# Reordering a two-layer streaming encoder into one-sequence blocks, with 64-row score pairs and denominators from ones columns beside V

## The chip, the cores and the metric

The kernel runs on one Trainium2 chip, on all 8 cores. Each core computes 2 of the 16 sequences and no core talks to another. The metric is device time in microseconds (us) of the slowest core. TensorE (PE in the profile) does the matmuls, VectorE is DVE, ScalarE is ACT, GpSimd is POOL and SyncE is SP.

Executions fall into two states. In the fast state the eight cores agree within about 0.5%. In the slow one, the cores of one or both dies show a lower granted TensorE clock and the run takes some per cent longer. Everything below compares fast runs, or the cores of an undisturbed die, unless it says otherwise.

## The reference

The model dimension is 1,024 and a sequence has 2,048 positions. In order: FFN, mixer A, FFN, FFN, mixer B, FFN. Cut and simplified to what matters:

```python
def rms_norm(x, g):
    y = x * lax.rsqrt(jnp.mean(x * x, axis=-1, keepdims=True) + EPS)
    return y * g
...
for layer in range(DEPTH):                       # DEPTH = 2
    h = h + 0.5 * swiglu(rms_norm(h, ffn1_norm[layer]), ...)      # hidden 2816
    hn = rms_norm(h, mix_norm[layer])
    if layer < N_A_LAYERS:                       # layer 0
        # 16 heads of 64; chunks of 64 see themselves and 8 chunks back,
        # with a bias by clipped relative distance
        h = h + chunked_relpos_attention(hn, ...)
    else:                                        # layer 1
        # 8 heads; scores = 128-row part + 64-row rotary part, block-causal
        h = h + mla_attention(hn, ..., k_nope, k_rope, v_shared, cos, sin)
    h = h + 0.5 * swiglu(rms_norm(h, ffn2_norm[layer]), ...)
    if layer == N_A_LAYERS - 1:
        # latent (256) and rotary key (64) from one norm of h, up-projected per head
        k_nope, k_rope, v_shared = mla_shared_kv(rms_norm(h, kv_norm), ...)
return rms_norm(h, final_norm)
```

## The kernel before

Activations lie transposed, model dimension on the partitions, in tiles of 512 positions; four tiles are a sequence. A stage runs over both sequences before the next stage starts. A small scheduler keeps one instruction list per engine, in program order, and puts a semaphore wait wherever data demands it. Program order on TensorE therefore decides what can hide what.

A norm is a load of 2 MB, one square of 4,096 columns on ScalarE, eight matmuls against a matrix of ones (which sum over partitions and spread the sum over all of them), two ScalarE steps, and eight VectorE products:

```python
def norm_core(x3, xR, C, gcol, out3, outR, n, sq, defer=None):
    ...
    sch.add('act', lambda e: e.activation(sq3[:, 0:C, :], x3, AF.Square), [xR], [sqR])
    ps, psR = P[7]
    for c in range(C):
        MM(ps[:], ones[:], sq3[:, c, :], c == 0, c == C - 1, [sqR, onesR], [psR])
    ...   # rs = exp(-0.5 * ln(ps / n + eps)), then out = x * gain * rs
```

Inside an FFN stage the norms of the second sequence hide in the first one's down projection. At the start of a stage, and of each mixer, they hide in nothing:

```python
# in a_stage (mixer A), setup
for sbl in range(4):
    load_norm(src, srcR, t0 + sbl, G_MIX[0], st['hn'][:, :, sbl * 512:(sbl + 1) * 512],
              st['hnR'][sbl], st['sq'])
```

Both mixers multiply the exponentials by V and then, in a second matmul of the same width, by ones, for the softmax denominators. This is mixer A; one projection bank (`P[1]`; a bank is one of the eight accumulators of 128 x 512 that the kernel allots to TensorE's results) serves all query, key and value groups, and each group is copied out before the next may start:

```python
def pv_(u):
    ...
    MM(po[:, c0:c1], v3[:, kt, :], pT[:, c0:c1], first, last, [vR, pTR], [poR])
    MM(pd[:, c0:c1], ones[:], pT[:, c0:c1], first, last, [onesR, pTR], [pdR])
    if last:
        RCP(rd_[pl, :], pd[pl, :], [pdR], [rdR], 'dve' if hh == 0 else 'act')
        ...   # ao = po * rd_
```

A head of mixer A has 64 rows. Its scores are computed with 128 rows by filling the other head's half of the query tile with zeros; B's rotary part does the same. Per head, B projects keys, values and queries with nothing else on TensorE, then runs its attention. The output projection follows as a separate step with a residual load and store of 1 MB per group of four.

The softmax here doesn't subtract the row's maximum and nothing guards it: scores larger than these inputs give would overflow.

## Time and profile before

| | before |
|---|---|
| first six runs | 7126.6 to 7717.8 us, median 7267.9 |
| profiled run | 7131.0 us, cores 7081 to 7130 us |
| matmuls per core | 29,858, streaming 13.41 M columns |
| start-to-start spacing, 512 / 128 columns | 216 / 55.6 ns |

The spacing comes from the order of time of the trace. It agrees with the Trainium skill, "TensorE: Matmul & The Clock Gate", Part 1 ("Wait — 56ns, not 53.3ns?"): columns divided by 2.4 GHz plus about 2.5 ns. That formula is used below to say how much time a list of matmuls *must* take; I call this work. Before: 13.41 M / 2,400 per us + 29,858 × 2.5 ns = about 5,660 us. The remaining 1,470 us of 7,131 are waits, and time lost to half clock after waits.

First the page of the profile before. The second line is busy time per engine, the third the granted clock in 40 slices in tenths, the last the chain that ended last.

```profile
span 7129.5 us, 85828 instructions; the slowest of 8 cores (7081.2 to 7129.5 us)
PE 5934.0 (83%) x29282; PEld 2774.7 (39%) x29856; DVE 1893.9 (27%) x2488; ACT 1819.8 (26%) x2947; POOL 364.6 (5%) x1502
...
PEclk9999998997999899998999998799979997999897
...
PE 59%; DMA 21%; DVE 8%; ACT 6%; issue 4%; SPq 1%; POOL 0%; DVEq 0%; ACTq 0%; POOLq 0%; another core or an unknown queue 0%
```

PE reads 83% busy, but it counts the tail of each matmul's pipeline, so it is more than the work. The chain is the better warning: TensorE explains only 59% of the way to the end, DMA 21%. The clock dips in the slices where mixers start, and in some others. Next, what TensorE waited for (name of what it waited for, microseconds in total, number of waits, longest):

```profile
PE ps L383 <- ACT arena L431: 621.1, 64, 32.7
PE ps L383 <- DVE rr L469: 111.1, 62, 7.7
PE ps L383 <- DVE xn L650: 96.1, 15, 10.1
```

L431 is the square of a norm, L469 the residual add of the FFN, L650 that of a mixer. The squares in turn wait for loads:

```profile
L431 ACT ACTIVATE arena<-xn 128x4096 bf16<-128x4096 f32 (+2 forms) x80 | 261.6, 3270 | 1642.8 <-DMA xn<-xs 1433.8
L390 DVE RECIPROCAL rstd<-ps 64x512 f32<-64x512 f32 x64 | 214.4, 3350 | 106.1 <-PE ps L383 105.7
```

That is 1,434 us of ScalarE idleness ended by a load from DRAM, and a 3.35 us reciprocal, 64 times. Last, four stretches of the trace (span of the window, its length, busy time of PE, PEld, DVE, ACT, POOL, granted clock, DMA share, GB/s):

```profile
71.00:433.00 362.00, 360.21 (x1640) 163.87 (x1672) 73.26 (x106) 58.65 (x92) 12.67 (x24) 1.00 0.31 65
1043.00:1147.00 104.00, 42.20 (x221) 19.65 (x225) 34.63 (x48) 20.80 (x13) 0.53 (x1) 0.69 0.28 90
1147.00:1596.00 449.00, 382.39 (x2946) 228.74 (x3000) 232.08 (x225) 255.03 (x512) 73.08 (x463) 1.00 0.10 22
4386.00:4637.00 251.00, 122.38 (x435) 47.99 (x444) 100.83 (x140) 67.69 (x52) 2.64 (x5) 0.74 0.29 85
```

An FFN up projection keeps TensorE full (360 of 362 us at clock 1.00). The start of a mixer A sequence has it 42 of 104 us at clock 0.69, that of B's 122 of 251 at 0.74. This is where the time lies.

### The profile page before, as it was taken

What the parts mean: (1) busy time and instruction counts of PE and PEld (TensorE: products, weight loads), DVE (VectorE), ACT (ScalarE), POOL (GpSimd) and SP (SyncE); (2) the same over time, 40 slices, a digit from 0 to 9 for tenths busy, and PEclk for the clock granted to TensorE, in tenths of its full rate; (3) what the DMA queues carried; (4) which work ended last, traced back from release to release, by engine and by line L of the source; (5) the groups of instructions that cost most, each with busy time, mean ns of one, the idle gap of its engine ahead of it and who ended that gap; (6) DMA issues with size and microseconds to landing.
All of it is one profiled execution on the core that took longest, in us unless ns stands there. A gap on an engine that the chain in (4) does not pass through costs nothing.

```text
span 7129.5 us, 85828 instructions; the slowest of 8 cores (7081.2 to 7129.5 us)
## 1 busy us (share of the span) xinstructions
PE 5934.0 (83%) x29282; PEld 2774.7 (39%) x29856; DVE 1893.9 (27%) x2488; ACT 1819.8 (26%) x2947; POOL 364.6 (5%) x1502
## 2 busy tenths in 40 slices
PE   6999977885887799997998996588847886998795
PEld 2444433542553344443443442244313442443342
DVE  2222114552553212111212112322242112112212
ACT  2111103551553211110211111255324551111201
POOL 0000000110111000000000000000000000000000
PEclk9999998997999899998999998799979997999897
DMA  4242251014013425225325234211331116244335
GB/s 105 41 130 55 52 131 39 19 25 148 19 34 87 113 40 134 51 56 140 70 56 131 39 74 125 68 28 27 101 128 24 28 32 180 39 84 124 99 76 156
DMA packets 220021, 553.57 MB, mean 78 GB/s; under 512 B 18640, under 2 KB 18640, under 8 KB 211408
## 3 DMA queue, kind: packets, MB, share of 16 engines
q1 hardware_dynamic: 171936, 375.49, 16.4%
q0 software_dynamic: 47664, 172.54, 14.8%
q8 instruction: 254, 4.16, 0.2%
q14 instruction: 167, 1.37, 0.1%
HBM read 603.05 MB, written 117.44 MB: 101 GB/s over the span
## 4 chain that ended last, share of the span: by engine, by line
PE 59%; DMA 21%; DVE 8%; ACT 6%; issue 4%; SPq 1%; POOL 0%; DVEq 0%; ACTq 0%; POOLq 0%; another core or an unknown queue 0%
PE ps L383 59%; DMA rr<-xs 10%; DMA xn<-xs 4%; DMA rr<-xT 4%; ACT arena L431 2%; DVE rr L469 2%; DVE arena L449 2%; DMA xs<-xn 2%; ACT arena L777 1%; SPq L393 1%; DVE rstd L390 1%; ACT arena L992 1%; ACT arena L955 1%; DMA xn<-xT 1%; ACT rstd L440 0%
## 5 line engine op out<-in xcount | busy, mean ns | idle before, releaser
L383 PE MATMUL ps<-arena,wbf 128*128 128x512 bf16 (+1 forms) x20430 | 4629.1, 384 | 370.3 <-DVE rr L469 111.1
L383 PEld LDWEIGHTS ps<-arena,wbf 128*128 128x128 bf16 (+1 forms) x20864 | 2047.6, 99 | 2893.5 <-issue 587.1
L383 PE MATMUL ps<-arena,ones_sb 128*128 128x512 bf16 (+3 forms) x2100 | 711.2, 383 | 636.9 <-ACT arena L431 621.1
L383 PE MATMUL ps<-arena 128*128 128x512 bf16 (+3 forms) x3584 | 882.2, 325 | 129.0 <-POOL arena L782 32.9
L512 DVE TENSOR_TENSOR arena<-sg,ps 128x512 bf16<-128x512 f32 x704 | 483.1, 687 | 1896.4 <-PE ps L383 1837.7
L510 ACT ACTIVATE sg<-ps 128x512 f32<-128x512 f32 x704 | 420.4, 597 | 2009.0 <-PE ps L383 1906.0
L431 ACT ACTIVATE arena<-xn 128x4096 bf16<-128x4096 f32 (+2 forms) x80 | 261.6, 3270 | 1642.8 <-DMA xn<-xs 1433.8
L383 PEld LDWEIGHTS ps<-arena 128*128 128x128 bf16 x3712 | 358.2, 98 | 529.7 <-issue 278.7
L777 ACT ACTIVATE arena<-ps,cvec_sb 128x512 bf16<-128x512 f32 (+3 forms) x896 | 432.0, 525 | 458.7 <-PE ps L383 429.9
L383 PEld LDWEIGHTS ps<-arena,ones_sb 128*128 128x128 bf16 x2112 | 217.5, 105 | 816.1 <-issue 745.2
L449 DVE SCALAR_TENSOR_TENSOR arena<-xn,gains_sb,rstd 128x512 bf16<-128x512 f32 x512 | 384.2, 750 | 493.1 <-ACT rstd L442 450.8
L469 DVE SCALAR_TENSOR_TENSOR rr<-ps,rr 128x512 f32<-128x512 f32 x256 | 177.1, 692 | 1204.6 <-DMA rr<-xs 824.9
L409 POOL DMA_DIRECT2D wbf<-wblob x330 | 174.3, 528 | 5005.7 <-PE ps L383 4828.1
L992 ACT ACTIVATE arena<-ps 128x512 bf16<-128x512 f32 (+3 forms) x640 | 326.0, 531 | 189.1 <-PE ps L383 183.7
L390 DVE RECIPROCAL rstd<-ps 64x512 f32<-64x512 f32 x64 | 214.4, 3350 | 106.1 <-PE ps L383 105.7
L383 PE MATMUL ps<-arena,ident_sb 128*128 128x256 bf16 (+1 forms) x608 | 153.4, 254 | 34.0 <-DVE arena L736 31.5
L1012 DVE TENSOR_TENSOR arena<-ps,rstd 128x512 bf16<-128x512 f32 x64 | 44.3, 692 | 515.2 <-ACT rstd L388 509.3
L383 PE MATMUL ps<-wbf,arena 128*128 128x128 bf16 x2560 | 167.8, 222 | 9.3 <-DVE arena L708 7.7
L383 PEld LDWEIGHTS ps<-wbf,arena 128*128 128x128 bf16 x2560 | 154.9, 99 | 40.3 <-issue 19.5
L650 DVE TENSOR_TENSOR xn<-ps,xn 128x512 f32<-128x512 f32 x128 | 88.5, 691 | 255.1 <-PE ps L383 130.2
L440 ACT ACTIVATE rstd<-ps,eps_sb 128x512 f32<-128x512 f32 x80 | 55.0, 687 | 300.0 <-PE ps L383 289.1
L801 DVE TENSOR_TENSOR arena<-ps,rstd 64x512 bf16<-64x512 f32 x128 | 88.2, 689 | 137.2 <-ACT rstd L388 130.5
(38 smaller groups left out, 1022.2 us busy)
## 6 DMA issues: line engine op xcount, KB each, us to landing
xn<-xs SPq DMA_DIRECT2D x56, 2048.0 KB, 9.5
wbf<-wblob POOLq DMA_DIRECT2D x216, 512.0 KB, 5.2
xs<-rr SPq DMA_DIRECT2D x256, 256.0 KB, 2.5
rr<-xs SPq DMA_DIRECT2D x192, 256.0 KB, 4.0
wbf<-wblob POOLq DMA_DIRECT2D x64, 704.0 KB, 7.1
xn<-xs SPq DMA_DIRECT2D x32, 1024.0 KB, 6.9
xs<-xn SPq DMA_DIRECT2D x32, 1024.0 KB, 9.1
xn<-xT SPq DMA_DIRECT2D x8, 2048.0 KB, 10.1
```

The source lines that it names most:

```text
L383: sch.add('pe', lambda e: e.matmul(out, lhsT, rhs, start=start, stop=stop), rd, wr)
L390: sch.add('dve', lambda e: e.reciprocal(out, in_), rd, wr)
L409: sch.add('pool', lambda e: e.dma_start(out=wb[:, 0:w], in_=src), [], [wbR], 'wq%d' % bi)
L431: sch.add('act', lambda e: e.activation(sq3[:, 0:C, :], x3, AF.Square), [xR], [sqR])
L449: sch.add('dve', lambda e: e.scalar_tensor_tensor(out3[:, c, :], x3[:, c, :], gains[:, gcol + c:gcol + c + 1], rs[:], ALU.mult, ALU.mult), ...
L469: sch.add('dve', lambda e: e.scalar_tensor_tensor(r[:], po, scale, r[:], ALU.mult, ALU.add), [poR, rR], [rR])
L510: sch.add('act', lambda e, sgt=sgt, pg=pg: e.activation(sgt[:], pg[:], AF.Silu), [pgR], [sgR])
L512: sch.add('dve', lambda e, av=av, sgt=sgt, pu=pu: e.tensor_tensor(av, sgt[:], pu[:], ALU.mult), [sgR, puR], [st['actR'][s]])
L650: sch.add('dve', lambda e, r=r, po=po: e.tensor_tensor(r, po[:], r, ALU.add), [poR, xR], [xR])
L777: sch.add('act', lambda e: e.activation(pT[:, c0:c1], sp_[:, c0:c1], AF.Exp, bias=cvec[:, h:h + 1]), [spR, cvR], [pTR])
L801: sch.add('dve', lambda e: e.tensor_tensor(ao[pl, a, QB * 512:(QB + 1) * 512], po[pl, :], rd_[pl, :], ALU.mult), [poR, rdR], [st['aoR'][QB]])
L992: sch.add('act', lambda e: e.activation(pT[:, c0:512], sp_[:, c0:512], AF.Exp, scale=scale), [spR], [pTR])
```

## The change

The intent has four parts:

1. **One-sequence blocks.** The order becomes F0 F0 A A F1 F1 F2 F2 B B F3 F3, each block one sequence (FFN of sequence 0, FFN of sequence 1, and so on), written F00, F01, A0, A1, F10, … below. The norm of block n+1 runs as background steps in the tail of block n: beside the down projection of an FFN, beside the last head and output projection of a mixer. B's shared latent and rotary key are made in the tails of F11 and F20 ("KV blocks").
2. **Row-tiled scores.** A's two heads of 64 rows go to the two halves of the array as a pair, and so do B's rotary parts of two key tiles. No zero padding.
3. **Denominators for free.** A's V tile for one head is 64 columns of V and 64 of ones, so one matmul gives both. B turns its product over: the exponentials are the stationary operand, V with a ones column (129 columns) streams past, and the result, query-major, is transposed back.
4. **Projection of the next head inside the current one**, in small groups between attention units; output projections by tile, with 256 KB residual loads and stores through a ring of four buffers.

The core of the diff (2,086 lines in all):

```diff
@@ the norm of the next block as a list of steps @@
+        def norm_steps(jobs, overlap=True):
+            ...
+            for n, j in enumerate(jobs):
+                ...
+                if n < 2:
+                    out.append(j.load)
...
@@ ffn_block, down projection @@
+            kv = blk in KV_IN
+            if next_jobs:
+                bg.q = norm_steps(next_jobs)
...
+                        rs.add(i, t0 + s, po, poR, 0.5)
+                        bg.step(4 if kv else 2)
...
@@ the KV steps of a norm job @@
+                if kv:
+                    tail += [knrm(0), knrm(1), knrm(2), knrm(3), nop, kmm(0), kmm(1), krope, ksq, nop, kst, kfin]
...
@@ mixer A, scores @@
-                        MM(sp_[:, c0:c1], kT[:, kt * 128:(kt + 1) * 128], qT[:, hh, QB * 512 + c0:QB * 512 + c1],
-                           True, not has_g, [kR, qR], [spR])
...
+                for hh in range(2):
+                    sp_, spR = P[b0_ + hh]
+                    pl = slice(hh * 64, hh * 64 + 64)
+                    MM(sp_[:, c0:c1], k_[ks][0][pl, kc:kc + 128], q_[QB][0][pl, c0:c1], not has, True,
+                       [k_[ks][1], q_[QB][1]], [spR], skip=True)
...
@@ mixer A, product with V @@
-                        MM(po[:, c0:c1], v3[:, kt, :], pT[:, c0:c1], first, last, [vR, pTR], [poR])
-                        MM(pd[:, c0:c1], ones[:], pT[:, c0:c1], first, last, [onesR, pTR], [pdR])
...
+                for hh in range(2):
+                    po, poR = P[4 + hh]
+                    MM(po[:, c0:c1], va[:, kt % 4, hh, :], pt[:, hh, c0:c1], first, last, [vr, ptR], [poR])
+                if last:
+                    rd_, rdR = rstd[nxt('rstd', 2)]
+                    ACT(rd_[0:64, :], P[4][0][64:128, :], AF.Ln, [P[4][1]], [rdR])
+                    ACT(rd_[64:128, :], P[5][0][0:64, :], AF.Ln, [P[5][1]], [rdR])
+                    ACT(rd_[:], rd_[:], AF.Exp, [rdR], [rdR], scale=-1.0)
...
@@ mixer B, product with V, query-major @@
+                    for qt in range(max(k - 4 * Q, 0), 4):
+                        po, poR = P[4 + qt // 2]
+                        cc = (qt % 2) * 256
+                        MM(po[:, cc:cc + 129], pt[:, i, qt * 128:(qt + 1) * 128], vh[k // 4][0][:, k % 4, 0:129],
+                           k == 0 and qt % 2 == 0, k == 4 * Q + qt, [vh[k // 4][1], ptR], [poR], skip=True)
...
@@ residual ring @@
+                dma(xview(dst, i, sb), r[:], [rR], [dstR[sb][i]], 'rs%d' % k)
+                self.ahead(self.order.index((i, sb)) + 4)
```

## The prediction

> **What bounds it now.** TensorE is busy 5934 of 7130 us (first part of the page), which counts pipeline tails. The order of time shows a 512-column matmul starting every 216 ns, a 128-column one every 55.6 ns. The 29,858 matmuls stream 13.41 M columns, so TensorE needs about 5,660 us. The other 1,470 us are waits, plus half clock after them (948 us at 0.5 in the clock record). The waits view: TensorE waits 621 us for squares of norms (which wait for loads), 111 us for FFN residual adds, 96 us for mixer residual adds. The stage windows: FFN runs at pace (first one 972 us against 925 of work); mixer A takes about 1,275 us against 865 of work, mixer B 1,580 against some 1,000. Norms and projections around the head loops run TensorE 40 to 55% busy at clock 0.7 to 0.78.
>
> **What changes, counted from both instruction lists.**
> 1. Columns fall to 12.61 M: the ones matmuls for denominators go (A 287 k, B 279 k; B's query-major product adds 2 k and 33 k of transposes); the rotary query's two 64-column passes become one. Same spacings: 5,330 us, 330 less.
> 2. A's scores and B's rotary scores become 64-row pairs. If pairs run side by side (the Trainium skill, "TensorE: Matmul & The Clock Gate", Part 3, says row tiles do; no run here shows it), 282 k columns vanish: -118 us. But "TensorEngine Tiling (Array Packing)", Key Properties, says that changing tiling mode drains TensorE. This trace agrees: switching between 128*128 and 128*64 matmuls spaces 310 ns, not 216: 94 ns more. 768 units x 2 switches x 94 ns = +144 us. Net about zero.
> 3. Norms, KV projection and output projections move into tails or beside the last head. Their sources are already stored, blocks being ordered by sequence. Most of the 621, 111 and 96 us and the half clock goes.
> 4. Exponentials cover two heads or key tiles (from 594 ns per 512 columns to an estimated 1.02 us per 1,024); 3.35 us reciprocals go.
>
> **New costs.** A has one output bank pair, freed after Ln, Ln, Exp and two multiplies, about 3.9 us; two projection groups (3.5 us) cover it. Output projection loads follow their stores on one queue with four buffers, so back-to-back groups take about 2.7 us instead of 1.73: 10 to 15 us per mixer block. The KV chain has five dependent hops per tile: 5 to 8 us x 8.
>
> **Sum (estimate).** Start 55; FFN 3,700 with norms; KV 14 + 50; A 2 x 440; B 2 x 450; final tail 12; about 5,620 us undisturbed. The before median is 2% above its fastest runs; I allow a little for that.
>
> Predicted: 5650 us, range 5450 to 5900. Faster by over 2%: 0.97; within 2%: 0.02; slower: 0.01.
>
> **What shows it right.** Waits for norm squares under 60 us; half clock under 150 us; FFN blocks of 455 to 480 us; A near 440 and B near 450 us per sequence; row pairs starting within 10 ns of each other, 94 ns lost per mode switch; the chain of waits almost all TensorE.
>
> **What would make it wrong.** Row pairs that do not overlap (+118 us); dearer switches (each 100 ns more is +154 us); weight loads of the query-major product not hidden[...]; background DVE or ACT work holding up exponentials; denser TensorE work that lowers the granted clock (at 0.94 throughout, +350 us).

## The result, and the profile after

The changed kernel takes 5920.6 us (median of ten runs; the eight fast ones are 5911.8 to 5926.6 us). Beside it the kernel before took 7170.9 us (median of 20 runs). The ratio is 0.8294, with a 95% interval of 0.8273 to 0.8315. Ratios here are the mean time of one kernel's fast runs over that of the other's in the same rounds, so not quite the ratio of the medians.

So it is 17% faster, and still 270 us slower than predicted, 21 us above the range.

The same four parts of the page, after:

```profile
span 5916.7 us, 83304 instructions; the slowest of 8 cores (5889.9 to 5916.7 us)
PE 5500.0 (93%) x29784; PEld 2580.6 (44%) x29784; DVE 1785.1 (30%) x2784; ACT 1571.7 (27%) x2313; POOL 293.4 (5%) x1053
...
PEclk9999999999999999999999899999998999999999
...
PE 83%; DMA 5%; DVE 5%; ACT 3%; issue 2%; SPq 0%; DVEq 0%; ACTq 0%; POOL 0%; POOLq 0%
```

The chain is now TensorE for 83%, and the clock is full nearly everywhere. What TensorE still waits for:

```profile
PE ps L381 <- ACT sq L384: 147.3, 28, 35.5
PE ps L381 <- DVE arena L396: 47.5, 25, 7.2
PE ps L381 <- DVE rr L387: 45.5, 13, 13.3
PE ps L381 <- DVE arena L387: 43.6, 76, 3.0
PE ps L381 <- DVE sq L390: 42.2, 8, 6.9
PE ps L381 <- ACT arena L384: 24.0, 41, 2.4
```

In order: squares of norms, copies of a projection out of its bank, residual adds of the mixers, multiplications (in A those that free the output bank), the products of a KV tile, and exponentials. The 621 us of squares became 147, of which 35.5 is the very first load of the program. The residual adds of the FFN are no longer among the larger waits.

### Accounting by block

I split each block's span by the spacing from start to start of the matmul records: *work* (columns/2.4 GHz + 2.5 ns, a row pair counted once), *switch* (what a change of tiling mode adds), *cold* (what half clock adds to a spacing), and *wait* (the rest). This is my own arithmetic on the trace, not a view of the profile. A few waits below are sums by this spacing too, which come out up to 0.2 us per wait longer than the waits view (48 us for the residual adds where the view has 45.5; 116 us for squares inside the blocks where it has 111.8).

| block, after | span us | work | switch | cold | wait |
|---|---|---|---|---|---|
| F01, F10, F21, F30, F31 (each) | 466 to 483 | 463 to 470 | 0 | 0 to 3 | 2 to 8 |
| F00 (its span includes 35.5 before the first matmul) | 541 | 470 | 0 | 4 | 32 |
| A0, A1 (each) | 471 | 349 | 44.5 | 8 | 69 |
| F11, F20 (KV; each) | 535, 538 | 485 | 0 | 11 | 39, 43 |
| B0, B1 | 504, 497 | 375 | 32 | 17, 15 | 79, 75 |
| all twelve and the ends | 5,917 | 5,209 | 153 | 81 | 430 + 44 at the ends |

Before, the same arithmetic gives the two A sequences together 879 of work and 360 of wait in 1,272 us, and the two B sequences 1,066 and 415 in 1,565 us (the shared keys are inside B there). These are from core 1, whose trace holds all matmuls; the records of the slowest core lack 574 of them, and what is missing would count as wait.

The KV block's loss can be read in the order of time of the trace, here in F11 (start, duration, engine, line, what it made from what; in brackets idle time before, and what ended it):

```profile
2767.04 6.73 DVE L390 SCALAR_TENSOR_TENSOR sq<-xn,gains_sb,rstd 128x512 bf16<-128x512 f32 x8
...
2774.03 7.51 PE L381 MATMUL ps<-sq,wbf 128*128 128x512 bf16 x24 [5.47 <-DVE sq L390]
...
2783.60 1.48 DVE L387 TENSOR_TENSOR xn<-ps,xn 64x512 f32<-64x512 f32 x2 [9.23 <-DMA xn<-tabT]
2785.18 1.06 ACT L384 ACTIVATE sq<-xn 128x1024 bf16<-128x1024 f32 x1 [4.61 <-DVE xn L387]
...
2786.38 0.59 PE L381 MATMUL ps<-sq,ones_sb 128*128 128x512 bf16 x2
```

Eight products on VectorE take 6.73 us, more than the FFN group of 22 matmuls (4.75 us) that TensorE has beside them, and TensorE waits 5.47 us. After that its 24 matmuls take 7.51 us where 5.2 would do: for the first 4.5 us or so they run at half clock. Then the rotary products at 2783.60 wait for a load of their table, the square at 2785.18 waits for them because it reads the tile that they write, and the sum at 2786.38 waits for the square. That is one tile of eight. Each such handing over from one engine to the next is called a hop below.

The mixer's tail, here the end of A0:

```profile
1453.99 0.37 SPq L378 DMA_DIRECT2D xn<-xs  x1
...
1458.34 0.53 POOL L426 DMA_DIRECT2D wbf<-wblob  x1 [13.63 <-PE ps L381]
...
1461.80 0.53 POOL L426 DMA_DIRECT2D wbf<-wblob  x1 [2.92 <-PE ps L381]
...
1475.41 0.69 DVE L387 TENSOR_TENSOR rr<-ps,rr 128x512 f32<-128x512 f32 x1 [13.18 <-DMA rr<-xs]
...
1476.25 3.57 PE L381 MATMUL ps<-arena,wbf 128*128 128x512 bf16 x8 [13.33 <-DVE rr L387]
```

At 1453.99 a 2 MB load for the next norm is issued. At 1458 and 1461.8 two weight loads are issued on another queue. The residual tile that the add at 1475.41 needs had its load issued at 1456.08; it landed 19 us later, and TensorE stood 13.3 us. The window around it shows what the 16 DMA engines were doing:

```profile
1456.00:1475.00 19.00, 6.92 (x33) 2.94 (x30) 4.11 (x6) 3.59 (x5) 1.05 (x2) 0.81 0.96 234
```

Their busy share is 0.96, at 234 GB/s, while TensorE worked 6.9 of 19 us.

### The profile page after: what moved, and what is told of

It is laid out like the page before. It is cut to its first block, busy times and chain, and to the rows that moved or that the text cites. A ratio compares the mean times of both kernels' runs of the same rounds, so it can differ in the third digit from the quotient of the medians.

```text
span 5916.7 us, 83304 instructions; the slowest of 8 cores (5889.9 to 5916.7 us)
## 1 busy us (share of the span) xinstructions
PE 5500.0 (93%) x29784; PEld 2580.6 (44%) x29784; DVE 1785.1 (30%) x2784; ACT 1571.7 (27%) x2313; POOL 293.4 (5%) x1053
## 4 chain that ended last, share of the span: by engine, by line
PE 83%; DMA 5%; DVE 5%; ACT 3%; issue 2%; SPq 0%; DVEq 0%; ACTq 0%; POOL 0%; POOLq 0%
PE ps L381 83%; DVE hn L390 2%; DMA xn<-xs 2%; ACT rstd L384 2%; DVE arena L387 1%; DMA xs<-rr 1%; ACT sq L384 1%; DMA rr<-xs 1%; DMA xn<-xT 1%; DVE sq L390 1%; DMA xn<-tabT 0%; ACT arena L384 0%; SPq L378 0%; PE ps L1220 0%; DMA hn<-tabT 0%
## 5 line engine op out<-in xcount | busy, mean ns | idle before, releaser
L381 PE MATMUL ps<-hn,wbf 128*128 128x512 bf16 x13440 | 2951.7, 380 | 36.6 <-DVE xn L396 13.6
L381 PEld LDWEIGHTS ps<-hn,wbf 128*128 128x128 bf16 x13440 | 1310.7, 98 | 1600.1 <-issue 67.2
L381 PE MATMUL ps<-arena,wbf 128*128 128x512 bf16 (+1 forms) x6520 | 1449.8, 381 | 66.5 <-DVE rr L387 40.9
L381 PEld LDWEIGHTS ps<-arena,wbf 128*128 128x128 bf16 x6520 | 639.7, 99 | 821.9 <-issue 110.4
L384 ACT ACTIVATE arena<-ps 128x1024 bf16<-128x1024 f32 (+5 forms) x896 | 607.9, 695 | 849.8 <-PE ps L381 796.2
L381 PE MATMUL ps<-arena 128*128 128x129 bf16 (+8 forms) x5248 | 727.5, 283 | 85.4 <-DVE arena L387 38.6
L381 PEld LDWEIGHTS ps<-arena 128*128 128x128 bf16 (+1 forms) x5248 | 306.2, 96 | 494.8 <-issue 426.9
L384 ACT ACTIVATE sq<-xn 128x1024 bf16<-128x1024 f32 (+2 forms) x296 | 274.8, 929 | 586.7 <-DMA xn<-xs 231.2
L390 DVE SCALAR_TENSOR_TENSOR hn<-xn,gains_sb,rstd 128x512 bf16<-128x512 f32 x432 | 323.4, 749 | 130.9 <-ACT rstd L384 100.2
L396 DVE CAST arena<-ps 128x512 bf16<-128x512 f32 x384 | 259.2, 689 | 310.5 <-PE ps L381 303.8
L381 PE MATMUL ps<-wbf,hn 128*128 128x128 bf16 x2048 | 128.0, 222 | 12.3 <-DVE arena L396 12.3
```

What stands on the lines that cost most here:

```text
L381: sch.add('pe', lambda e: e.matmul(out, lhsT, rhs, start=start, stop=stop, skip_group_check=skip), rd, wr)
L384: sch.add('act', lambda e: e.activation(out, in_, func, **kw), rd, wr)
L390: sch.add('dve', lambda e: e.scalar_tensor_tensor(out, a, sc, b, op0, op1), rd, wr)
L396: sch.add(eng, lambda e: e.tensor_copy(out, in_), rd, wr)
```

## The experiments

My theory, after reading the trace: work and mode switches are about as predicted (5,209 + 153 against 5,212 + 144), and the whole error is waiting. The waits fall into five groups: late norm loads, the KV hops, the output bank in A, residual tiles in the mixer tails, and copies at the start of a mixer. Rivals: a switch costs more than its spacing shows (then undoing the row pairs gains); the waits hide other limits behind them (then removing one only moves it); and the tail of a mixer is slow because of bulk loads beside it, or because of the ring that feeds it. Where the expectations say theory A and B, they define them each time for that run. Diffs are against the changed kernel. All kernels that I call correct agreed with the reference within its tolerance.

### 1. Norm loads issued earlier

```diff
+        def hoist(js):
+            for j in (js or [])[:2]:
+                j.load()
+                j.load = nop
...
+                if j == NJ - 4:          # FFN: three weight tiles before the tail
+                    hoist(next_jobs)
...
+                    if a == 6:           # A, and h == 6 in B: one head earlier
+                        hoist(next_jobs)
```

> The first two 2 MB loads of the next block's norms are issued well before the tail (four weight tiles before the end of the up products, or one head before the last) instead of at its beginning; nothing else changes. Theory A (the loads are issued only 10 to 19 us before the first statistics need the squares, and land after 11.5 us, so the squares come late): TensorE's wait for squares of norms falls from 147 us to about 55 (what remains is the start of the kernel), half clock falls by some 30 to 50 us, and the time from 5918 to between 5815 and 5850. Rival B (the squares are late because ScalarE is busy or behind in its order): less than 15 us gained, the waits stay.

Measured: correct. Five of six runs fell in the slow state; the one fast run is 5856.8 us, and the undisturbed dies of the slow ones show 5827 to 5855 us per core, against 5890 to 5917 in the profile after. That is about 61 us less. On an undisturbed core plain FFN blocks fall to 462.7 us with no wait at all, the waits for squares inside the blocks from 116 to 31 us, and time at half clock from 290 to 214 us. The A blocks did not gain: they took 477 and 474 us. The waits view of that undisturbed core (core 1):

```profile
PE ps L381 <- ACT sq L384: 65.2, 17, 36.9
```

So late loads were the cause in FFN blocks. In A there was little to gain: squares end only 9.2 us of the waits of its two blocks in the profile after, and in A0 the first two loads of the next norm were already issued at 1237 and 1238 us for a sum at 1390 us.

### 2. The KV chain spread, one hop per FFN group

```diff
-                    tail += [knrm(0), knrm(1), knrm(2), knrm(3), nop, kmm(0), kmm(1), krope, ksq, nop, kst, kfin]
+                    return head[:4], [[st, nrm(0), nrm(1)], [nrm(2), nrm(3), knrm(0)], [knrm(1), knrm(2), knrm(3)],
+                                      [], [kmm(0), kmm(1), krope], [ksq], [kst, kfin]], None
...
-                        bg.step(4 if kv else 2)
+                        bg.step(1 if kv else 2)
```

> In the two FFN blocks that also make the shared keys and values, the background steps are dealt out one set per down group of 22 matmuls, so that each hop that TensorE waits for (scaled rows, squares of the latent) has a group or more between it and its user; the work is the same. Theory A (the 135 us that the two blocks cost over a plain one, where I had estimated 64, are dependent hops issued with no TensorE work between them): the two blocks fall from 535 and 538 to about 490 to 500 us, the time to between 5825 and 5850. Rival B (VectorE or the queue has not the throughput for the extra work in this tail): under 20 us gained, VectorE is still what TensorE waits for.

Measured: correct, fast runs 5848.6 and 5850.9 us, ratio 0.8182 (0.8167 to 0.8198) against 0.8294. The two KV blocks fell from 535 and 538 us to 499 and 498, and the wait for their products (42.2 us in the profile after) is gone. The hops were the main cause, and an FFN group (4.75 us) between two of them covers them. They were not the only one: run 1, which left the hops as they were, took about 16 us off each of these blocks, so late norm loads had a part in them too.

### 3 and 4. Row pairs undone, in A and in B

```diff
 # A: both heads' query tiles padded with zeros again
-                        CP(q_[s][0], pp, [ppR], [q_[s][1]])
+                        for hh in range(2):
+                            pl = slice(hh * 64, hh * 64 + 64)
+                            CP(q_[s][hh][0][pl, :], pp[pl, :], [ppR], [q_[s][hh][1]])
...
-                    MM(sp_[:, c0:c1], k_[ks][0][pl, kc:kc + 128], q_[QB][0][pl, c0:c1], not has, True,
-                       [k_[ks][1], q_[QB][1]], [spR], skip=True)
+                    MM(sp_[:, c0:c1], k_[ks][0][:, kc:kc + 128], q_[QB][hh][0][:, c0:c1], not has, True,
+                       [k_[ks][1], q_[QB][hh][1]], [spR], skip=True)
```

> Mixer A's scores go back to full 128-row products with a zero-padded query (two copies of 64 partitions each), so there is no row tiling and no mode switch in A; all else is as in the kernel after. Theory A (896 switches of about 100 ns cost 89 us, the pairs save only 60): the time falls by 15 to 35 us, to 5885 to 5905; work in A rises from 349 to about 380 us per sequence, switches go to zero. Rival B (switches are hidden in waits that would be there anyway, so that row tiling is a net gain): the time rises by 30 to 60 us.

Measured: correct, fast runs 5914 to 5945 us, ratio 0.8297 (0.8283 to 0.8311). That is no change, where both theories had expected one: a miss. The profiled run, with both dies at a granted clock of 0.82, can't show where the gain went; it shows only that the switches are gone. What ate it stays open. More copies on VectorE is a guess that no fast trace shows.

```diff
 # B: the second half of the rotary key (rows 64 to 127) set to zero, full 128 rows
-            dma(kr[64:128, :], kr_d[:, t0 * 512:(t0 + 4) * 512], [krR_d[t0 + s] for s in range(4)], [krR2], 'kl1')
+            PSET(kr[64:128, :], 0.0, [krR2])
...
-                    MM(sp_[:, c0s[i]:512], kr[pl, k * 128:(k + 1) * 128], qr[Q][0][pl, c0s[i]:512], False, True,
+                    MM(sp_[:, c0s[i]:512], kr[:, k * 128:(k + 1) * 128], qr[Q][0][:, c0s[i]:512], False, True,
```

> Mixer B's rotary scores go back to 128-row products (the second half of the rotary key rows is zeroed instead of a second copy of the key), no row tiling in B; all else as in the kernel after. Theory A (640 switches of about 100 ns cost 64 us, the pairs save 58): the time changes by less than 12 us, rather down. Rival B (switches hidden in waits): it rises by 30 to 58 us.

Measured: correct, 5910.7 to 5911.2 us, ratio 0.8268 (0.8255 to 0.8281): about 7 us less, as expected. In a B block work rises from 375 to 406 us and switches fall from 32 to 0. The pair saves about what the switch costs.

Together the two say that row tiling was worth nothing here, as the prediction had it ("net about zero").

### 5. A's output bank freed in two halves

```diff
                 if last:
-                    rd_, rdR = rstd[nxt('rstd', 2)]
-                    ACT(rd_[0:64, :], P[4][0][64:128, :], AF.Ln, [P[4][1]], [rdR])
-                    ACT(rd_[64:128, :], P[5][0][0:64, :], AF.Ln, [P[5][1]], [rdR])
-                    ACT(rd_[:], rd_[:], AF.Exp, [rdR], [rdR], scale=-1.0)
                     for hh in range(2):
                         pl = slice(hh * 64, hh * 64 + 64)
+                        dl = slice(64 - hh * 64, 128 - hh * 64)
+                        rd_, rdR = rstd[nxt('rstd', 2)]
+                        ACT(rd_[pl, :], P[4 + hh][0][dl, :], AF.Ln, [P[4 + hh][1]], [rdR])
+                        ACT(rd_[pl, :], rd_[pl, :], AF.Exp, [rdR], [rdR], scale=-1.0)
```

> In mixer A the reciprocals of the two heads are taken one after the other (Ln, Exp, multiply for head 0, then the same for head 1) instead of Ln, Ln, one Exp over both, then two multiplies; one more ScalarE instruction per query block, 64 in all. So the first output bank is free about 1.3 us sooner. Theory A (the 27 us per A block that TensorE waits for the output multiply are the single pair of output banks, freed 3.9 us after the last product while the two filler groups cover only 3.5 us): that wait falls from 53 us in both blocks to under 15, the time to about 5875 to 5895. Rival B (VectorE is behind with the fillers' copies, so that the multiply is late whenever the reciprocal comes): under 12 us gained.

Measured: 5902.2 and 5906.9 us, about 14 us less, but a wrong result. That was my slip: with two buffers used per round, the split overwrites a norm's inverse root that a later step still reads. The order of work on each engine is the intended one, so the time still tells something. It tells against the theory: the wait for the output bank did not fall below 15 us, it *rose*, from 43.6 to 64.4 us by the waits view, while the waits for exponentials fell from 24.0 to 7.0:

```profile
PE ps L381 <- DVE arena L387: 64.4, 64, 4.2
...
PE ps L381 <- ACT arena L384: 7.0, 15, 0.8
```

All eight cores agree (61 to 65 us for the bank, 39 to 44 before). The wait moved from one name to another on the same path.

### 6. The starts of the mixers

```diff
-            bias_make(0)
             for g in proj(0):
                 g()
+            bias_make(0)
...
+            MISC_B = [2, 3, 6, 7]
...
-            g0 = proj(0)
+            g0 = proj(0, MISC_B, 'act')
```

B's first projections use four banks instead of two and are copied out by ScalarE.

> Two changes at the starts of mixer blocks. In A the bias rows, whose load lands 9 us into the block, are scaled after the first projections and not before, so that VectorE's copies of queries and keys are not queued behind that load. In B the copies of the first head's projections go to ScalarE, idle there for 30 us, and the down and first projections use four PSUM banks and not two. Theory A (VectorE's order, not its throughput or TensorE, holds up the starts): A's wait of 7 and 5 us for copies goes, B's of about 27 us per block for copies and down projections falls to under 12; the time to about 5870 to 5890. Rival B (the start of B is bound by the table loads and the rotary chain on VectorE): under 15 us gained.

Measured: correct, 5889.1 and 5890.9 us: 29 us less. A0 fell to 465 us and B0 and B1 to 490 and 486. Copies ended 22.3 us of waits instead of 47.5, but the waits for squares rose by 17 us: part of what is freed at the start is spent again later.

```profile
PE ps L381 <- DVE arena L396: 22.3, 21, 1.4
```

### 7. Norm loads in four pieces, and a residual ring of five

```diff
-                dma(self.x3, xfull(src, sb), list(srcR[sb]), [self.xR], 'xn%d' % k)
+                cc = slice(2 * q, 2 * q + 2)
+                dma(self.x3[:, cc, :], xfull(src, sb)[:, cc, :], srcR[sb][cc], [self.xR[q]], 'xn%d_%d' % (self.k, q))
```

> The norm loads of 2 MB are issued as four of 512 KB, and those of the third and fourth tile of a block one by one behind the steps that free their part of the buffer; rows and bytes are the same. Theory A (the residual loads of 256 KB in the output projection tails wait behind a 2 MB load on the same queue: one took 18.6 us to land at 1454 us and TensorE then waited 13.3 us): TensorE's wait for mixer residual adds falls from 48 us to under 20, waits for squares fall too since the first piece lands early, the time to about 5850 to 5885. Rival B (what I wrote in the prediction: stores before loads on one queue with four buffers limit the pace): those waits stay above 35 us.

Measured: correct, 5860.6 and 5865.1 us: 56 us less, a gain of the expected kind for a different reason. The residual waits were to fall and hardly did (48 to 40 us on the profiled core; over all eight cores the view gives 42 to 46 us before and 38 to 47 after). The gain came from the norms themselves: F00 fell from 541 to 520 us, because the first square can start when a quarter of the load is there, and the waits for squares fell from 147.3 to 108.2 us.

```diff
-        rr = [(sb_alloc("rr%d" % i, [128, 512], F32), R()) for i in range(4)]
+        rr = [(sb_alloc("rr%d" % i, [128, 512], F32), R()) for i in range(5)]
...
-                self.ahead(self.order.index((i, sb)) + 4)
+                self.ahead(self.order.index((i, sb)) + 5)
```

> The ring of residual buffers grows from four to five and loads run five ahead (a sixth does not fit). Theory A (2 MB loads ahead in the queue hold up the residual loads): little is gained, waits for mixer residual adds stay above 35 us of 48, the time within 12 us of 5918. Rival B (the store-before-load pace with four buffers): they fall in proportion, to below 25 us, and the time to about 5885 to 5900.

Measured: correct, 5922.5 and 5968.8 us (the second, which is the profiled one, with a slightly low clock on one die): no gain. The waits of TensorE in that kernel:

```profile
PE ps L381 <- ACT sq L384: 186.5, 31, 36.8
...
PE ps L381 <- DVE rr L387: 13.0, 7, 3.6
```

The residual wait fell from 45.5 to 13.0 us, and the wait for squares rose from 147.3 to 186.5. This core is on the disturbed die; the four cores of the other die show the same, with 15 to 28 us for residuals and 152 to 187 for squares, where the eight cores of the changed kernel have 42 to 46 and 131 to 147. A deeper ring does take much of the residual's wait away, but the squares then wait longer by about as much. That both compete for the same DMA engines is my reading of it; the next but one group of experiments looks at that.

### 8. What hiding the norms is worth

```diff
+            if n and blk[:2] != ('F', 2):
+                cur['misc'] = MISC_A
+                for g in norm_steps(jobs):
+                    g()
...
-                a_block(blk, jobs, src, srcR, dst, dstR, nj)
+                a_block(blk, jobs, src, srcR, dst, dstR, None)
```

Everything else stays, but norms run at the start of their own block, as before the change (F2's stay in the tails, with the KV steps).

> The kernel after with the norms of nine of the eleven later blocks taken out of the tail before them and run at the start of their own block, with nothing beside them (the two blocks that make keys and values keep theirs); same instructions, same columns. Theory A (hiding the norms is the largest part of what the change gained: they cost the kernel before about 55 us per block, 621 us of waits for squares in all): the time rises by 380 to 500 us, to 6300 to 6420, with half clock near 600 us. Rival B (the gain came from fewer columns and a denser head loop, the norms' waits being replaced by waits in the tails): under 200 us lost.

Measured: correct, 6320 to 6326 us: 402 us more, within what was expected.

```profile
PE ps L381 <- ACT sq L384: 506.2, 54, 36.3
```

The waits for squares are back at 506 us, and time at half clock is 669 us. So about 400 of the roughly 1,210 us gained come from moving norms into tails. By the accounting, 451 us come from fewer columns (118 of them the row pairs). The rest, after 150 us are lost to switches, comes from projections, residuals and KV no longer running alone; I did not take these apart one by one.

### 9. The mixer's tail: whose loads are in the way?

First the 2 MB norm loads of the last two tiles are left out in mixer tails. The result is wrong (relative error 0.275).

```diff
-                dma(self.x3, xfull(src, sb), list(srcR[sb]), [self.xR], 'xn%d' % k)
+                if not (sch.tag[:1] in ('A', 'B') and sb % 4 >= 2):
+                    dma(self.x3, xfull(src, sb), list(srcR[sb]), [self.xR], 'xn%d' % k)
```

> Wrong results on purpose: in the tails of the four mixer blocks the third and fourth 2 MB norm load of the next block are left out, so those two norms read what the buffer holds; all else is issued as before. Neither smaller pieces nor a fifth buffer moved the mixer tails: with five buffers the residual waits fell from 48 to 24 us but waits for squares rose by as much. Theory A (in these tails the 16 DMA engines are full: 84% busy at 210 GB/s over the last 46 us of the first A block, 96% at the worst, so the bytes themselves are what TensorE waits for): TensorE's wait for mixer residual adds falls from 48 to under 15 us, the time to 5850 to 5885. Rival B (the residual's own chain of store, load and add sets the pace): the waits stay above 35 us, and under 15 us are gained.

Measured: 5896 to 5904 us, 20 us less; the residual waits fall only from 48 to 39 us. In the trace, residual transfers still take 9 to 18 us to land after three 768 KB weight loads issued within 7 us. So the weight loads matter at least as much as the norm loads. Two more kernels were to hold the weight loads back to the end of the block, one of them with the norm loads left out too:

```diff
-        def w_done(name):
+        def w_done(name, fill=True):
             wstate['free'].append(wstate['at'][name].pop(0))
-            w_fill()
+            if fill:
+                w_fill()
...
             bg.flush()
+            w_fill()
```

> In the tails of the mixer blocks the next block's weight tiles are fetched one (two before the second B block) as the output projection frees its buffers, the others only at the block's end. In the run without tail norm loads the stores and loads of residuals, 2.4 to 5 us to landing until then, took 9 to 18 us from the moment three weight tiles of 768 KB were issued (1457 to 1464 us). Theory A (any bulk load in these tails holds up the residuals; taking one kind away leaves the other): alone it gains little, waits for mixer residual adds 30 to 48 us, time within 20 us of 5918. Rival B (the weight tiles alone are the cause): these waits fall below 15 us, the time to about 5870 to 5885.

> Wrong results on purpose: both at once, no third and fourth norm load in the mixer tails and the weight tiles late. Theory A (bulk loads of either kind hold up the residuals): TensorE's wait for mixer residual adds falls from 48 to under 15 us, more than the two runs give separately, and the time to 5850 to 5880. Rival B (the residual's own chain of store, load and add on one queue, as in my prediction): it stays above 30 us.

Measured: the first 5923.7 us and correct (ratio 0.8283, 0.8252 to 0.8314), the second 5890 and 5901 us (wrong, ratio 0.8244), the same as without the norm loads alone. These are null experiments. The first one's trace shows weight loads issued at 1456, 1459 and 1478 us, where the changed kernel has 1458, 1462 and 1480; the second one's at 1460, 1463 and 1467 us, where the run without norm loads has 1457, 1461 and 1464. They are nearly where they were: the load was moved to the end of POOL's *program order*, but POOL does nothing else then, and the load waited only for its buffer. Order in a list holds nothing back; only a dependency does. So again, with a dependency on the block's last VectorE instruction:

```diff
+            endR = R()
+            endR.lw = sch.ops['dve'][-1]
+            w_fill([endR])
```

> The run with late weights did not do what it said: the fetches stood at the block's end in program order but waited for nothing there, and the trace shows them issued at 1460, 1463 and 1467 us as before. Now they wait for the last VectorE instruction of the block. Theory A (any bulk load in the tails holds up the residuals; the norm loads remain): waits for mixer residual adds 25 to 48 us, the time within 20 us of 5918. Rival B (the weight tiles alone are the cause): waits below 15 us, time 5870 to 5885.

> Wrong results on purpose: no third and fourth norm load in the mixer tails, and the weight tiles really held to the block's end. Theory A (bulk loads of either kind hold up the residuals): no residual transfer in the last 40 us of a mixer block takes over 8 us, TensorE's wait for mixer residual adds falls from 48 to under 15 us, the time to 5850 to 5880. Rival B (the residual's own chain of store, load and add with four buffers): the wait stays above 25 us though the transfers are quick.

Measured: weights held, correct, one fast run of 5909.7 us, 9 us under the profiled run and just under the lowest of the changed kernel's other fast runs (5911.8), so the time alone shows little. Held and without norm loads (wrong), 5878.6 and 5885.3 us (and 5896.0 with a low clock on one die), ratio 0.8242 (0.8212 to 0.8272): 35 us less. The residual line of the waits view, weights held:

```profile
PE ps L381 <- DVE rr L387: 30.3, 15, 7.4
```

and with neither (profiled in the run with the low clock):

```profile
PE ps L381 <- DVE rr L387: 22.5, 13, 3.3
```

From 45.5 us (longest 13.3) to 30.3 and 22.5 (longest 3.3). Over all eight cores of each run it is 42 to 46, 26 to 31 and 19 to 22 us, so the steps are clear of the spread, and of the low clock. The last is neither under 15 us, as theory A had it, nor above 25, as its rival had it. In the last 40 us of the four mixer blocks, 12 of 73 residual transfers took over 8 us to land in the changed kernel, 1 of 95 with neither. So bulk loads on the same DMA engines cause the long gaps and about half of the wait. The other half remains with nothing beside it; it comes in many gaps of up to 3 us, which fits the ring's own pace (a store, then a load, per group), but no run shows that alone. It stays open.

### 10. What worked, together

The version combines 1 (in FFN and B only), 2, 4, 5 (with separate buffers, so correct), 6, 7's pieces, and in its last form weights held in mixer tails.

> All that helped, together: early norm loads before FFN and B tails, the key and value steps spaced, loads in four pieces, both mixer starts, reciprocals head by head (in other tiles than before, which mends the wrong result of that run: a norm's scale factors had been overwritten), B's rotary scores without row tiling. If the gains are separate (61, 69, 55, 29, 14 and 7 us, less some 50 that two of them claim twice, and 15 because A's early loads are left out): about 5735 to 5785 us. If they only pass one wait on to the next: above 5815.

> The best version so far (5715 us) with the weight tiles of the mixer tails late. Theory A: with the norm loads in pieces, the residuals' waits fall from 45 to about 25 us, the time to 5690 to 5710. Rival B: no change within 8 us, or slower, because the next block then waits for its weights.

> The best version so far (5715 us) with the weight tiles held to the end of the mixer blocks. Theory A: the residuals' waits fall from about 50 to about 30 us, the time to 5690 to 5710. Rival B: no change within 8 us, or slower, because the next block then waits for its weights.

Measured: the first form 5715.0 and 5715.1 us and correct (5752 with one die slightly disturbed), 20 us better than the expected 5735 to 5785. The second added the weight edit that holds nothing back, and gave 5711.1 and 5711.6: the same. The last form gave 5696.6 us undisturbed (5730 and 5757 with slightly lower clocks), correct, ratio 0.8041 (0.7987 to 0.8096). The step from 5711 rests on this one undisturbed run. Its 5696.6 us are 3.7% below the changed kernel's profiled run of 5918.3 us; by the ratios, whose fast runs include the two slightly disturbed ones, it is 3.1%.

```profile
span 5695.0 us, 84197 instructions; the slowest of 8 cores (5673.9 to 5695.0 us)
PE 5441.9 (96%) x29784; PEld 2625.3 (46%) x29784; DVE 1765.7 (31%) x2760; ACT 1626.4 (29%) x2401; POOL 296.7 (5%) x1055
...
PEclk9999999999999999999999999999999999999999
```

```profile
PE ps L381 <- ACT sq L384: 61.1, 21, 32.1
PE ps L381 <- DVE arena L387: 59.7, 61, 4.1
PE ps L381 <- DVE rr L387: 31.6, 15, 6.7
PE ps L381 <- DVE arena L396: 29.1, 24, 2.0
```

By the block accounting, waits are 253 us (from 430) and cold is 42 (from 81). The largest that is left inside the blocks is A's output bank (59.7 us; of the 61.1 for squares, 32.1 are the first load). Even so the time stays above the 5,620 us of the predicted sum.

## Why the prediction was right or wrong

**Direction and mechanism: right.** Faster, by moving norms and projections beside other work and by fewer columns; the chain became 83% TensorE, where "almost all" was predicted.

**Work: right.** 5,330 − 118 = 5,212 us predicted, 5,209 measured.

**Row pairs: right.** The second of a pair starts 3 ns after the first, which agrees with the Trainium skill, "TensorE: Matmul & The Clock Gate", Part 3 (about 4 ns). A switch into row tiling spaces 312 ns and out of it 318 ns, not 216: 96 and 103 ns, where 94 was predicted; 153 us in all against 144. "TensorEngine Tiling (Array Packing)", Key Properties, says that a change of tiling mode drains TensorE; this agrees. Its "up to 2×" under "Theoretical Speedup" did not come: 153 us of switches against 118 us saved, and two experiments that undo the pairs change the time by 0 and −7 us.

**Exponentials: right.** An exponential over 1,024 columns takes 1,022 ns (304 of them, groups of the profile after); the estimate was 1.02 us.

**FFN blocks: nearly right.** 455 to 480 predicted, 466 to 483 measured for the plain ones.

**The failed step is the sum of waits.** The total of 5,620 us leaves 264 for all waits, half clock, start and end, after work and switches. The trace shows 555 (430 + 81 + 44). This one term was sized at half; its 291 us are nearly all of the error of 297 us against the sum. Its parts, against the prediction's words:

- "The KV chain has five dependent hops per tile: 5 to 8 us x 8". Measured: the two KV blocks together take 135 us more than two plain ones, where the sum had 14 + 50. About 45 of the 135 are the KV matmuls themselves (485 us of work in each block against 463), so the waits and half clock are about 90, or 11 us per tile. I took each hop for a latency that an FFN group mostly covers. The trace shows a run of eight products (6.73 us) that is longer than the group beside it, a table load and a chain of short hops behind it, and half clock after the longest wait. Spreading them took 69 us away: shown. Part of the 90 was late norm loads, as run 1 shows.
- "B 2 x 450": 504 and 497, 101 us too little together. I had no term for B's starts (copies out of two banks) nor for its half clock. A change of those starts took about 12 us off each B block: shown for that part; the rest of B is not settled (the view of the two B blocks has 35.2 us for copies, 26.6 for squares and 18.2 for residual adds).
- "A 2 x 440": 471 each, 62 too little. Two projection groups were to cover the output bank; they did not. Freeing it in halves moved the wait to itself from the exponentials and gained 14 us. What would remove it is not shown. Nor is it the whole miss: of the waits of the two A blocks the view puts 43.6 us down to multiplications that free this bank, 27.3 to residual adds, 22.2 to exponentials, 12.3 to copies and 9.2 to squares.
- "Waits for norm squares under 60 us": 147. Tails were assumed to hide loads wholly, but in FFN tails the first two loads were issued only 10 to 19 us before use, at the very start of the tail. Issuing them earlier took 61 us away: shown in FFN, whose five plain blocks, the end of the program left out, together took 2,351 us, 39 over five eighths of the predicted 3,700. "Start 55" was 79: F00 takes 541 us against the 462 of an FFN block that waits for nothing, and 35.5 of them are the first load.
- "Half clock under 150 us": 290. I made the condition and gave no term of the sum to it. It costs 81 us, and it is not a cause of its own: each of the 39 stretches of half clock before the end of the trace stands beside an idle gap of TensorE of 2.2 us or more.
- "10 to 15 us per mixer block" for residual loads was the right size (45.5 us in four blocks, 11 each), with half of the reason. I named the store before the load and four buffers. A fifth buffer did shorten this wait, and lengthened another; but the long gaps come from bulk loads on the same DMA engines, which I had not named, and holding them back halved the wait.

**What the warnings did.** Weight loads of the query-major product are hidden (129 columns space 57 ns). The granted clock in the profiled run is 0.976, and its clock record holds nothing but full clock and half clock beside waits.

## What to carry to other kernels

When work is moved into a tail to hide it, budget its loads as well as its matmuls: issue them a whole step earlier, and count who else uses the DMA engines in that tail. A chain of dependent hops costs only what its gaps exceed; one full group of matmuls between two hops hides a hop, and a whole step's worth of VectorE products between them does not fit. When a list of waits is long, take the sum of all small ones from the trace of a similar stage rather than from the best case of each, and expect a removed wait to come back in part under another name.

## What the Trainium skill lacked or had wrong

- "TensorEngine Tiling (Array Packing)", Key Properties, says that switching mode drains TensorE and gives no cost. Here it is 96 ns into 64-row tiling and 103 ns out of it for 512-column matmuls, 153 us over the program, more than the 118 us that the pairs save; its "Theoretical Speedup" should say that the cost of the switches has to be taken off.
- "TensorE: Matmul & The Clock Gate", Part 2, "Back-to-back issue gap", gives a sustained spacing with weight loads of about 81 ns at 128 columns and 131 ns at 512. Here streams with a new weight load for every matmul space 55.6 ns (57 for 129 columns) and 216 ns, the values that it calls isolated.
- The same page, Part 1, says to budget 13/16 of the clock whenever three cores or more of a die run dense matmuls. Here all eight run dense throughout, and the clock record of the changed kernel's profiled run, slowest core, holds only 1.0 (5,577 us) and 0.5 (290 us). The 13/16 is real: the slow profiled run of the kernel with A's pairs undone holds exactly 0.8125 for 6,071 us on its slowest core. It comes in some executions and not in others (2 of the 10 runs of the changed kernel, and it came for the kernel before too), and nothing here shows what decides it.
- "DMA: Bandwidth & Descriptors", "Issuing engines are not separate DMA queues", says that queues share the 16 engines and interleave. This agrees, but no number says what a small transfer pays: 256 KB residual loads with a median of 4.1 us to landing took up to 19 us while 768 KB weight loads and a 2 MB load from other issues ran, at a DMA busy share of 0.96.
